# An opening computed feature chunk by feature chunk, and projections spread over the attention steps

## The chip, the cores and the metric

The kernel runs on one core of a Trainium2 chip. The metric is the device time of one execution in microseconds (us); three runs of the kernel before gave 2430.28, 2433.61 and 2434.09 us, so the median is 2433.61 us. The engines are named as the profile names them: PE multiplies matrices and PEld loads its weights, DVE works on vectors, ACT evaluates functions, POOL is the general engine, and SP issues most of the transfers.

## The reference, cut to what matters

Two networks run one after the other. The change lies in the first one, a transformer of two layers over 256 tokens `x` and 256 context tokens `ctx`, 1024 features each. All values are 32-bit floats.

```python
for l in range(DEPTH):                       # DEPTH = 2
    with_ctx = l < DEPTH - 1
    mod_x = (silu_c @ w_ada[l] + b_ada[l])[:, None, :]      # six modulation vectors of 1024
    mod_c = (silu_cc @ w_ada[l] + b_ada[l])[None, None, :]
    sh1_x, sc1_x, gt1_x, sh2_x, sc2_x, gt2_x = jnp.split(mod_x, 6, axis=-1)
    ...
    hx = modulate(rms_norm(x, g_norm1[l]), sh1_x, sc1_x)    # h * (1 + scale) + shift
    hc = modulate(rms_norm(ctx, g_norm1[l]), sh1_c, sc1_c)
    qa, ka, va, qb, kb, vb, qc, kc, vc = jnp.split(hx @ w_in[l], bounds, axis=-1)
    ...                                      # the same for hc; three kinds of attention: a, b, c
    x = x + gt1_x * (jnp.concatenate([oa, ob, oc], axis=-1) @ w_out[l])
    hx2 = modulate(rms_norm(x, g_norm2[l]), sh2_x, sc2_x)
    x = x + gt2_x * conv_ffn(hx2, w_up[l], conv_w[l], conv_b[l], w_down[l])
    ...                                      # the same for ctx while with_ctx
```

The second network (two layers of feed-forward, attention, linear attention, feed-forward) takes `x` from there.

## The kernel before, in words

Features lie on the 128 partitions in eight chunks, tokens lie along the free dimension; both streams together make 512 columns. Every large product runs in three parts: `weight` (L254) loads a 512 KB weight tile, ACT rounds it to a high part (L261), DVE makes the low part (L262), and `mm1` (L265) issues the products high by high, high by low and low by high at L269, L270 and L271. One output tile of 128 features over eight chunks is therefore 24 matmuls.

*Opening* (`first`, from L791 on). SP loads the streams H and C, constants and vectors, and then `w_ada`. `ada` (L362) is a generator of steps: one step loads 512 KB of `w_ada` into one of the four weight buffers and multiplies it by the two condition vectors (L372); eight steps make one of the six modulation vectors of a layer. Sixteen steps, the shift and the scale of layer 0, run in the opening. ACT squares both streams (L339), DVE and POOL add them, PE sums them over the partitions (L350, L351), ACT and DVE make the factor of the norm (L315 to L324). DVE multiplies the streams by it (L820, L821), and when the sixteenth step is through, `modulate` (L417) makes the inputs of the projections.

*Projections and attention* (`first_layer`). Layer l has 18 projection tiles, in the order of `IN1` (L56). `gemm` (L279) runs the first three chunk by chunk side by side and the next three one after the other; `done` then normalises each query or key tile (L447 to L458, with a sum by PE at L450) or transposes values (L468). Tiles 6 to 17 come from the generator `project`. Eight attentions follow: two of kind c, two of kind b, four of kind a. An attention consists of steps: scores on PE (L528 for c, L531 and L532 for the others), a maximum on DVE (L478), exponentials on ACT (L480), a scaling on ACT (L491), transposes on PE (L551, L569), copies on DVE (L554), and at its end the product with the values (L579, L586). In layer 0 an attention has 6 steps, in layer 1 it has 4. Each step calls `fill` once: a projection while any are left, and after that a step of `ada`. After the attentions come the output projection, the second norm, and the feed-forward stage, whose 41 later tiles each call one more step of `ada`.

What sets the order: the program is written as above, and a scheduler then lines up each engine's instructions, with an eye to free buffers (four for weights, 33 named `n`, 18 named `q`, five PSUM banks `mm`, three PSUM banks `at`). On the chip each engine runs its line in order.

Of the kernel before, what the change touches and what calls it, by code (L numbers as in the profile page):

```python
# [9 lines left out]
F32 = mybir.dt.float32  # L10
# [29 lines left out]
_CON = [("ident", 128), ("ones", 128), ("ones128", 128), ("bd64", 128), ("bd32", 128), ("causal", 128)]  # L40
# [15 lines left out]
IN1 = ("kc", "vc", "qc", "kc", "vc", "qc", "kb", "vb", "qb", "kb", "vb", "qb", "ka", "va", "qa", "qa", "qa", "qa")  # L56
LEVELS = (64, 32, 16, 8, 4, 2, 1)


def _constants():  # L60
# [25 lines left out]
    put("causal", np.where(i[None, :] <= i[:, None], 0.0, MASKED))  # L86
    m = np.zeros((P, 8, P), np.float32)
# [10 lines left out]
def prep(v):  # L98
# [14 lines left out]
    d["w_ada"] = f(v["w_ada"])  # L113

# [71 lines left out]
class Kern:  # L186
# [92 lines left out]
    def gemm(self, tiles, done, head=3, hook=None, order=None, fill=None, ws=None):  # L279


        order = order or range(KC)
        ws = ws or [self.weight(t[0]) for t in tiles[:head]]
        pss = [self.mmp()[:, :t[2]] for t in tiles[:head]]
        for i, k in enumerate(order):
            for w, ps, t in zip(ws, pss, tiles):
                self.mm1(ps, w, k, t[1][k], i == 0, i == KC - 1)
        if hook:
            hook()
        for i, ps in enumerate(pss):  # L290
            done(i, ps)
# [125 lines left out]
    def modulate(self, l, v, gain, streams, zs, n, xn=None):  # L417
# [3 lines left out]
        for c in range(KC):  # L421
            hi, lo = self.n(F32R), self.n(F32R)
            if xn:
                t = self.t()[:, :512]
                for part, _ in streams:
                    u = slice(part * 256, (part + 1) * 256)
                    g, sh = gain[:, c, part:part + 1], self.mod(l, v, c, part)
                    nc.scalar.activation(hi[:, u], xn[c][:, u], AF.Identity, scale=g, bias=sh)
                    nc.vector.tensor_scalar(t[:, u], xn[c][:, u], g, sh, ALU.mult, ALU.add)
                nc.vector.tensor_tensor(lo, t, hi.bitcast(F32), ALU.subtract)  # L430
                xs.append((hi, lo))
                continue
# [173 lines left out]
    def first_layer(self, l):  # L606
# [7 lines left out]
        zs, head = None, self.head  # L614
        if not wc:
# [4 lines left out]
        xs = self.modulate(l, 0, self.G1[l], both, zs, 512, self.xn if wc else None)  # L620
        cut = {n: [(h[:, :n], o[:, :n]) for h, o in xs] for n in (256, 512)}
# [29 lines left out]
        self.gemm(tiles[:6], done, ws=head)  # L651
# [10 lines left out]
        self.project = project()  # L662
# [19 lines left out]
        order = []  # L682
        for j in range(2):
# [107 lines left out]
    def first(self, ctx):  # L791
# [15 lines left out]
        st = [self.stat_new(256, nc.vector), self.stat_new(256)]  # L807
# [3 lines left out]
        self.G1, self.G2 = {}, {}  # L811
        self.known, self.mods = -1, self.ada()
        for i in range(16):
            next(self.mods)
            if i == 7:
                with self.tc.issue_after(self.last_ada):
                    zs = [self.stat_end(s) for s in st]
                self.xn = [self.n() for _ in range(KC)]
                for c in range(KC):
                    nc.vector.tensor_tensor(self.xn[c][:, :256], self.H[:, c, TM:TH], zs[0], ALU.mult)  # L820
                    nc.vector.tensor_tensor(self.xn[c][:, 256:], self.C[:, c, :], zs[1], ALU.mult)  # L821
        self.head = [self.weight(A["w1_in"][0, j]) for j in range(3)]
        nc.sync.dma_start(self.CON1, A["con1"])
        nc.sync.dma_start(self.LAM, bass.AP(A["lamv"].tensor, 0, [[0, P], [1, 256]]))
# [476 lines left out]
_INS = ["hT", "cT", "ccT", "w_ada", "w1_in", "w1_out", "w1_up", "w1_dn", "w2_in", "w2_fg", "w2_out", "w2_up1", "w2_dn1",  # L1301
# [19 lines left out]
```

## Time and profile before

| | us |
|---|---|
| median of three runs | 2433.61 |
| the profiled execution | 2433.39 |
| its span, first to last instruction | 2431.6 |
| PE busy | 2320.8 (95%) |
| DVE busy | 1523.2 (63%) |
| ACT busy | 1270.2 (52%) |
| POOL busy | 401.7 (17%) |

The execution's own time is 1.8 us longer than the span. An engine's busy time is the time in which at least one of its instructions runs; PE's counts a matmul until it has left the array, so PE can be busy and still have gaps between starts. "Idle" below is the length of a stretch less the busy time.

### The profile page before, as it was taken

How to read it: one execution, taken by the hardware profiler on the slowest of the kernel's cores; microseconds unless marked ns; L12 is line 12 of the kernel's file. 1: busy time of each engine (PE TensorE's matmuls, PEld its weight loads, DVE VectorE, ACT ScalarE, POOL GpSimd, SP SyncE). 2: the span in 40 equal slices, each digit the busy share in tenths (PEclk: the TensorE clock that was granted, in tenths of full speed). 3: DMA queues.
4: the chain of work that ended last, by engine and by line, in shares of the span. 5: the costliest groups of instructions: out<-in, count | busy, mean ns of one | idle time of the engine just before them, and what ended most of it. 6: DMA issues, size and time to landing. Idle time of an engine off the chain costs nothing. (4 is left out here: it accounts for less than half of the span.)

```text
span 2431.6 us, 40872 instructions
## 1 busy us (share of the span) xinstructions
PE 2320.8 (95%) x16128; PEld 2043.5 (84%) x16128; DVE 1523.2 (63%) x2605; ACT 1270.2 (52%) x2196; POOL 401.7 (17%) x417
## 2 busy tenths in 40 slices
PE   5999999999999989999999999899999999998998
PEld 3665677778877758999999988899989999888997
DVE  4667665444547776776664876676466557666664
ACT  3658644333346775664444545554454444466553
POOL 0300021000022001211111320321121122113111
PEclk8999999999999999999999999999999999999999
DMA  7313335433233246556555533445545545334653
GB/s 269 103 37 131 113 130 173 139 121 96 93 117 120 71 156 211 194 177 191 183 168 180 167 106 105 148 157 174 174 148 178 169 147 195 104 114 149 196 180 118
DMA packets 100993, 358.57 MB, mean 147 GB/s; under 512 B 11488, under 2 KB 12864, under 8 KB 100544
## 3 DMA queue, kind: packets, MB, share of 16 engines
q1 hardware_dynamic: 98640, 349.82, 44.4%
q0 software_dynamic: 1792, 5.53, 0.9%
q8 instruction: 127, 2.08, 0.4%
q10 hardware_dynamic: 368, 0.59, 0.1%
q14 instruction: 66, 0.54, 0.1%
HBM read 354.83 MB, written 1.07 MB: 146 GB/s over the span
## 5 line engine op out<-in xcount | busy, mean ns | idle before, releaser
L269 PE MATMUL mm_t<-n_t,hi_t 128*128 128x272 f32 (+2 forms) x3600 | 1112.4, 310 | 25.4 <-ACT n_t L839 18.7
L270 PE MATMUL mm_t<-n_t,hi_t 128*128 128x272 f32 (+2 forms) x3600 | 1109.5, 308 | 6.0 <-DVE n_t L840 5.0
L271 PE MATMUL mm_t<-n_t,lo_t 128*128 128x272 f32 (+2 forms) x3600 | 1106.0, 308 | 1.1 <-DVE lo_t L262 1.1
L262 DVE TENSOR_TENSOR lo_t<-raw_t,hi_t 128x1024 fp32r<-128x1024 f32 (+1 forms) x574 | 713.2, 1246 | 391.2 <-ACT hi_t L261 387.1
L261 ACT ACTIVATE hi_t<-raw_t 128x1024 fp32r<-128x1024 f32 (+1 forms) x574 | 595.5, 1039 | 680.6 <-PE mm_t L270 509.4
L269 PEld LDWEIGHTS mm_t<-n_t,hi_t 128*128 128x128 f32 x3600 | 686.0, 191 | 77.7 <-ACT n_t L839 20.9
L270 PEld LDWEIGHTS mm_t<-n_t,hi_t 128*128 128x128 f32 x3600 | 688.5, 191 | 38.1 <-DVE n_t L840 8.4
L271 PEld LDWEIGHTS mm_t<-n_t,lo_t 128*128 128x128 f32 x3600 | 687.9, 191 | 33.0 <-issue 5.8
L269 PE MATMUL mm_t<-q_t,hi_t 128*128 128x272 f32 (+2 forms) x896 | 274.6, 307 | 0.7 <-ACT q_t L306 0.7
L270 PE MATMUL mm_t<-q_t,hi_t 128*128 128x272 f32 (+2 forms) x896 | 274.4, 306 | 0.0
L271 PE MATMUL mm_t<-q_t,lo_t 128*128 128x272 f32 (+2 forms) x896 | 274.3, 306 | 0.0
L343 POOL TENSOR_TENSOR t_t<-t_t 128x272 f32<-128x272 f32 (+1 forms) x108 | 122.9, 1143 | 540.2 <-ACT t_t L339 515.2
L269 PEld LDWEIGHTS mm_t<-q_t,hi_t 128*128 128x128 f32 x896 | 168.4, 188 | 8.8 <-ACT q_t L306 1.1
L270 PEld LDWEIGHTS mm_t<-q_t,hi_t 128*128 128x128 f32 x896 | 168.9, 188 | 7.6 <-DVE q_t L307 0.2
L271 PEld LDWEIGHTS mm_t<-q_t,lo_t 128*128 128x128 f32 x896 | 168.9, 189 | 7.5
L888 POOL TENSOR_TENSOR t_t<-t_t 128x272 f32<-128x272 f32 (+1 forms) x88 | 75.6, 860 | 443.3 <-DVE t_t L882 386.9
L738 POOL TENSOR_TENSOR t_t<-t_t 128x512 f32<-128x512 f32 (+1 forms) x44 | 56.7, 1288 | 442.2 <-ACT t_t L737 442.2
L882 DVE TENSOR_TENSOR t_t<-mm_t,t_t 128x272 f32<-128x272 f32 (+1 forms) x176 | 75.6, 436 | 64.2 <-PE mm_t L271 62.4
L372 PE MATMUL at_t<-raw_t,CS 128*32 128x256 f32 x768 | 70.6, 431 | 35.7 <-DMA raw_t<-in_w_ada_dram 35.4
L307 DVE TENSOR_TENSOR q_t<-t_t,q_t 128x272 fp32r<-128x272 f32 (+2 forms) x112 | 55.8, 498 | 73.4 <-ACT q_t L306 73.4
L306 ACT ACTIVATE q_t<-t_t 128x272 fp32r<-128x272 f32 (+2 forms) x112 | 52.3, 467 | 90.4 <-POOL t_t L738 47.8
L480 ACT ACTIVATE t_t<-mm_t,s_t 128x512 f32<-128x512 f32 (+1 forms) x120 | 72.7, 607 | 26.5 <-DVE s_t L478 25.7
(253 smaller groups left out, 2146.9 us busy)
## 6 DMA issues: line engine op xcount, KB each, us to landing
raw_t<-in_w_up_dram SPq DMA_DIRECT2D x264, 512.0 KB, 3.3
raw_t<-in_w_in_dram SPq DMA_DIRECT2D x118, 512.0 KB, 3.4
raw_t<-in_w_ada_dram SPq DMA_DIRECT2D x96, 512.0 KB, 4.4
raw_t<-in_w_dn_dram SPq DMA_DIRECT2D x96, 448.0 KB, 3.3
raw_t<-in_w_dn_dram SPq DMA_DIRECT2D x48, 512.0 KB, 3.6
raw_t<-in_w_out_dram SPq DMA_DIRECT2D x32, 512.0 KB, 3.4
raw_t<-in_w_fg_dram SPq DMA_DIRECT2D x16, 512.0 KB, 3.3
q_t<-cum POOLq DMA_DIRECT2D x8, 272.0 KB, 7.4
```

The source lines that it names most:

```text
L261: nc.scalar.activation(hi[:, :k], raw[:, :k], AF.Copy)
L262: nc.vector.tensor_tensor(lo[:, :k], raw[:, :k], hi[:, :k].bitcast(F32), ALU.subtract)
L269: self.nc.tensor.matmul(ps, wh, xh, start=start, stop=False)
L270: self.nc.tensor.matmul(ps, wh, xl, start=False, stop=False)
L271: self.last_mm = self.nc.tensor.matmul(ps, wl, xh, start=False, stop=stop).ins
L307: self.nc.vector.tensor_tensor(lo, src, hi.bitcast(F32), ALU.subtract)
L343: st.eng.tensor_tensor(st.acc, st.acc, sq, ALU.add)
L372: self.last_ada = nc.tensor.matmul(ps[32 * g:32 * g + 32], self.CS[:, k, :], wv[:, g], start=k == 0, stop=k == KC - 1).ins
L480: nc.scalar.activation(pm[:, i * nk:(i + 1) * nk], sp[:, i * nk:(i + 1) * nk], AF.Exp, bias=m[:, i:i + 1], accum_out=sm[:, i:i + 1])
L738: nc.gpsimd.tensor_tensor(u, u, g, ALU.mult)
L882: nc.vector.tensor_tensor(u, ps, z[0], ALU.mult)
L888: nc.gpsimd.tensor_tensor(u, u, g, ALU.mult)
```

## The change

There are three parts.

The first two modulations of layer 0 are no longer steps of `ada`. The host lays their part of `w_ada` out anew (`w_ada0`), so that 1 MB holds all that one chunk of 128 features needs of shift and scale. `ada_chunk` loads it in four transfers of 256 KB into `q` buffers and multiplies it (L436); `mod_chunk` turns the result onto the partitions by a small product with a selecting matrix (L447), makes shift and gain for this chunk, and applies norm and modulation in one pass. Two chunks are loaded ahead of H and C; the other six stand behind the first four weight tiles. `gemm` gets a `feed` that prepares a chunk just ahead of its products, and four tiles instead of three run side by side. Both streams' squares are added on DVE.

Projections in the attention are issued at the steps of the table `DUE` alone; every other step is a step of `ada`, and in layer 0 these run ahead into layer 1's modulations. In layer 0 two projections (tiles 6 and 7) run before the first attention.

```diff
+DUE = ((2, 4, 6, 8, 10, 12, 15, 18, 21, 28, 34, 40), (1, 2, 4, 5, 6, 8, 10, 12, 14, 18, 22, 26))
...
+    a = v["w_ada"][0, :, :2048].reshape(4, 2, P, 2, KC, P)
+    d["w_ada0"] = f(a.transpose(4, 0, 2, 1, 3, 5).reshape(KC, 4, P, 512))
...
         for i, k in enumerate(order):
+            if feed:
+                feed(k)
             for w, ps, t in zip(ws, pss, tiles):
                 self.mm1(ps, w, k, t[1][k], i == 0, i == KC - 1)
...
-        for l, v in ((l, v) for l in range(2) for v in range(6)):
+        for l, v in ((l, v) for l in range(2) for v in range(2 * (1 - l), 6)):
...
-        if next(self.project, None) is None:
-            self.ada_step(l, 4)
+        self.step += 1
+        if not (self.step in DUE[l] and next(self.project, None)):
+            self.ada_step(*(1, 1) if l == 0 else (1, 4))
...
+    def ada_chunk(self, c):
...
+        ps = self.atp()[:, :256]
+        for h in range(2):
+            ws = [self.q()[:, :512] for _ in range(2)]
+            for i, w in enumerate(ws):
+                self.last_dma = nc.sync.dma_start(w, self.A["w_ada0"][c, 2 * h + i]).ins
+            for g in range(4):
+                self.last_ada = nc.tensor.matmul(ps[32 * g:32 * g + 32], self.CS[:, 4 * h + g, :],
+                                                 ws[g // 2][:, g % 2 * 256:(g % 2 + 1) * 256], start=h == 0, stop=h == 1).ins
+        e = self.t()[:, :256]
+        nc.scalar.activation(e, ps, AF.Copy)
+        return e
+
+    def mod_chunk(self, c, e):
...
+        m = self.atp()[:, :4].rearrange("p (v s) -> p v s", v=2)
+        for v in range(2):
+            nc.tensor.matmul(m[:, v], e[:, v * P:(v + 1) * P], self.con("sel"), start=v == 0, stop=v == 1)
+        o, _ = _VOFF["b_ada"]
+        for v in range(2):
+            nc.vector.tensor_scalar(self.MOD[0][:, v * KC + c], m[:, v], self.VEC[:, o + v * KC + c:o + v * KC + c + 1], None,
+                                    ALU.add)
+        gain = self.G1[0]
+        nc.vector.tensor_scalar(gain[:, c], self.MOD[0][:, KC + c], 1.0, self.gh[:, c:c + 1], ALU.add, ALU.mult)
+        hi, lo, t = self.n(F32R), self.n(F32R), self.t()[:, :512]
+        for part, src in enumerate((self.H[:, c, TM:TH], self.C[:, c, :])):
+            u, sh = slice(part * 256, (part + 1) * 256), self.mod(0, 0, c, part)
+            nc.vector.scalar_tensor_tensor(t[:, u], src, gain[:, c, part:part + 1], self.zs[part], ALU.mult, ALU.mult)
+            nc.scalar.activation(hi[:, u], t[:, u], AF.Identity, bias=sh)
+            nc.vector.scalar_tensor_tensor(lo[:, u], t[:, u], sh, hi[:, u].bitcast(F32), ALU.add, ALU.subtract)
+        return hi, lo
...
+            def feed(k):
+
+                while len(sums) < min(k + 2, KC):
+                    sums.append(self.ada_chunk(len(sums)))
+                x = self.mod_chunk(k, sums[k])
...
+        if wc:
+            for _ in range(2):
+                next(self.project)
...
-        nc.sync.dma_start(self.H, A["hT"])
-        nc.sync.dma_start(self.C, A["cT"])
         nc.sync.dma_start(self.CON, A["con"])
-        nc.sync.dma_start(self.VEC, A["vec"])
...
+        self.sums = [self.ada_chunk(c) for c in range(2)]
+        with self.tc.issue_after(self.last_dma):
+            nc.sync.dma_start(self.H, A["hT"])
+            nc.sync.dma_start(self.C, A["cT"])
+            last = nc.sync.dma_start(self.VEC, A["vec"]).ins
+        st = [self.stat_new(256, nc.vector), self.stat_new(256, nc.vector)]
...
+        with self.tc.issue_after(last):
+            self.head = [self.weight(A["w1_in"][0, j]) for j in range(4)]
```

How the lines of instructions move is shown at three places, PE each time. Lines 269 to 271 of the kernel before are lines 275 to 277 after; `at_t` and `mm_t` are PSUM banks, and `CS` holds the two condition vectors.

PE before, from the sums of the norm to the first projection products:

```order
L350 MATMUL at_t<-t_t,CON 128x256
L351 MATMUL at_t<-t_t,CON 128x256
L372 MATMUL at_t<-raw_t,CS 32x256 x32
L269 MATMUL mm_t<-n_t,hi_t 128x512
L270 MATMUL mm_t<-n_t,hi_t 128x512
L271 MATMUL mm_t<-n_t,lo_t 128x512
```

PE after, the same stretch:

```order
L358 MATMUL at_t<-t_t,CON 128x256
L359 MATMUL at_t<-t_t,CON 128x256
L447 MATMUL at_t<-CON,t_t 128x2 x2
L436 MATMUL at_t<-q_t,CS 32x256 x8
L447 MATMUL at_t<-CON,t_t 128x2 x2
L436 MATMUL at_t<-q_t,CS 32x256 x6
L447 MATMUL at_t<-CON,t_t 128x2 x2
L436 MATMUL at_t<-q_t,CS 32x256 x2
L275 MATMUL mm_t<-n_t,hi_t 128x512 x3
L276 MATMUL mm_t<-n_t,hi_t 128x512
```

The second modulation's eight steps have left the place ahead of the first products; in their stead stand the sums of chunks 2 and 3 alone.

PE after, where the products of chunk 2 end and those of chunk 3 begin (before, the products of all eight chunks follow each other here):

```order
L277 MATMUL mm_t<-n_t,lo_t 128x512
L436 MATMUL at_t<-q_t,CS 32x256 x8
L447 MATMUL at_t<-CON,t_t 128x2 x2
L436 MATMUL at_t<-q_t,CS 32x256 x8
L447 MATMUL at_t<-CON,t_t 128x2 x2
L436 MATMUL at_t<-q_t,CS 32x256 x8
L447 MATMUL at_t<-CON,t_t 128x2 x2
L436 MATMUL at_t<-q_t,CS 32x256
L275 MATMUL mm_t<-n_t,hi_t 128x512 x2
```

The sums of chunks 4, 5 and 6 and an eighth of chunk 7's stand together in the middle of the products; the rest of chunk 7's stands ahead of the products of chunk 6.

PE before, in the first attention of kind b, layer 0, after its scores:

```order
L595 MATMUL at_t_1629<-t_t_1625,CON_81 128x512
L372 MATMUL at_t_1675<-raw_t_1676,CS_94 32x256 x4
L372 MATMUL at_t_1675<-raw_t_1701,CS_94 32x256 x4
L372 MATMUL at_t_1675<-raw_t_1728,CS_94 32x256 x4
L532 MATMUL mm_t_1743<-q_t_1652,q_t_1644 128x512
```

PE after, in the same attention (L566 and L567 are the scores; `mm_t_1650` is projection tile 14):

```order
L566 MATMUL mm_t_1630<-q_t_1561,q_t_1555 128x256
L567 MATMUL mm_t_1630<-q_t_1563,q_t_1555 128x256
L275 MATMUL mm_t_1650<-n_t_265,hi_t_1645 128x512
L276 MATMUL mm_t_1650<-n_t_266,hi_t_1645 128x512
L277 MATMUL mm_t_1650<-n_t_265,lo_t_1646 128x512
```

Where only steps of `ada` filled the line before, products of a projection now stand too. Counted over PE's whole line of layer 0, the steps of `ada` are 24 in the attentions, 6 in the wait of the second norm and 18 in the feed-forward stage before, and 38, 2 and 8 after. From the feed-forward stage of layer 1 on both lines are the same.

## Rows read from the trace of the kernel before

**Rows 1.** The page, busy us of each engine.
```profile
PE 2320.8 (95%) x16128; PEld 2043.5 (84%) x16128; DVE 1523.2 (63%) x2605; ACT 1270.2 (52%) x2196; POOL 401.7 (17%) x417
```

**Rows 2.** Stretches: length; busy PE, PEld, DVE, ACT, POOL; clock, DMA share, GB/s.
```profile
0.00:43.10 43.10, 17.02 (x137) 5.78 (x137) 15.03 (x51) 13.67 (x31) 4.82 (x10) 0.82 0.85 301
43.10:62.80 19.70, 18.79 (x74) 14.84 (x74) 14.53 (x30) 11.78 (x21) 0.00 (x0) 0.88 0.49 172
62.80:82.40 19.60, 19.60 (x83) 14.60 (x82) 13.29 (x20) 13.33 (x21) 4.76 (x4) 1.00 0.43 135
82.40:199.50 117.10, 109.47 (x488) 74.96 (x487) 78.72 (x161) 75.58 (x156) 21.39 (x24) 0.99 0.17 50
199.50:294.30 94.80, 86.67 (x631) 54.45 (x631) 73.71 (x175) 79.98 (x188) 1.41 (x2) 0.98 0.45 156
333.20:344.00 10.80, 7.99 (x62) 3.76 (x60) 7.37 (x19) 6.54 (x14) 0.00 (x0) 0.88 0.61 221
762.60:826.60 64.00, 60.29 (x295) 42.51 (x294) 47.53 (x99) 43.22 (x87) 17.03 (x18) 1.00 0.29 91
826.60:857.00 30.40, 26.54 (x204) 22.54 (x203) 21.41 (x56) 25.40 (x57) 4.69 (x7) 1.00 0.16 53
857.00:917.20 60.20, 56.34 (x405) 35.79 (x404) 43.07 (x114) 42.37 (x89) 1.42 (x2) 0.94 0.52 175
```

**Rows 3.** The same view, three stretches of the opening.
```profile
5.00:10.00 5.00, 0.00 (x0) 0.00 (x0) 0.00 (x0) 1.14 (x4) 0.00 (x0) 1.00 1.00 412
25.00:30.00 5.00, 4.58 (x39) 2.69 (x38) 2.35 (x8) 2.61 (x6) 0.00 (x0) 0.76 0.66 228
45.00:50.00 5.00, 5.00 (x16) 3.96 (x17) 5.00 (x10) 4.11 (x8) 0.00 (x0) 0.71 1.00 337
```

**Rows 4.** Timeline of the opening: start, length, instruction, idle time before.
```profile
9.28 0.42 ACT L339 ACTIVATE t_t<-C 128x256 f32<-128x256 f32 x1 [2.08 <-DMA C<-in_cT_dram]
...
13.97 0.42 ACT L339 ACTIVATE t_t<-C 128x256 f32<-128x256 f32 x1 [0.30 <-DVE t_t L343]
...
24.13 1.22 PE L350 MATMUL at_t<-t_t,CON 128*128 128x256 f32 x2
...
29.97 0.42 DVE L324 SCALAR_TENSOR_TENSOR t_t<-t_t 128x256 f32<-128x256 f32 x1
...
40.64 0.38 ACT L377 ACTIVATE t_t<-at_t 128x256 f32<-128x256 f32 x1 [11.45 <-PE at_t L372]
...
43.10 0.79 PE L269 MATMUL mm_t<-n_t,hi_t 128*128 128x512 f32 x1 [2.52 <-ACT n_t L428]
```

**Rows 5.** Timeline of PE: a projection, then two `ada` steps in layer 0's feed-forward.
```profile
180.10 0.40 PE L269 MATMUL mm_t<-n_t,hi_t 128*128 128x512 f32 x1
...
183.28 0.39 PE L271 MATMUL mm_t<-n_t,lo_t 128*128 128x512 f32 x1
...
365.41 0.64 PE L372 MATMUL at_t<-raw_t,CS 128*32 128x256 f32 x8
...
371.65 0.64 PE L372 MATMUL at_t<-raw_t,CS 128*32 128x256 f32 x8
```

**Rows 6.** Groups by line, PE, 199.5 to 294.3 us: count, busy, mean, idle before.
```profile
L372 PE MATMUL at_t<-raw_t,CS 128*32 128x256 f32 x192 | 16.3, 386 | 2.4 <-DMA raw_t<-in_w_ada_dram 2.3 <-DVE n_t L307 0.2
```

**Rows 7.** Waits of PE: us in total, times, longest; layer 0, then layer 1.
```profile
PE at_t L450 <- ACT t_t L447: 4.7, 6, 1.6
...
PE at_t L372 <- DMA raw_t<-in_w_ada_dram: 2.3, 5, 0.7
...
PE at_t L551 <- ACT t_t L491: 3.6, 2, 3.1
```

**Rows 8.** Groups by line, ACT and DVE, 82 to 294 us.
```profile
L261 ACT ACTIVATE hi_t<-raw_t 128x1024 fp32r<-128x1024 f32 x13 | 13.7, 1055 | 11.8 <-PE mm_t L270 11.6 <-DMA raw_t<-in_w_out_dram 0.2
L315 ACT ACTIVATE t_t<-at_t,eps 128x512 f32<-128x512 f32 x12 | 8.3, 688 | 6.5 <-PE at_t L450 5.5 <-PE at_t L595 0.8
L317 ACT ACTIVATE t_t<-t_t 128x512 f32<-128x512 f32 x12 | 7.5, 625 | 0.2
L320 DVE SCALAR_TENSOR_TENSOR t_t<-at_t,t_t 128x512 f32<-128x512 f32 x12 | 8.3, 690 | 6.2 <-ACT t_t L317 6.2
```

More of the change, by code (lines that the diff above doesn't have):

```diff
@@ L37 @@
 NVEC = _n
-_CON = [("ident", 128), ("ones", 128), ("ones128", 128), ("bd64", 128), ("bd32", 128), ("causal", 128)]
+_CON = [("ident", 128), ("ones", 128), ("ones128", 128), ("bd64", 128), ("bd32", 128), ("causal", 128), ("sel", 2)]
 _COFF = {}
@@ L86, in _constants @@
     put("causal", np.where(i[None, :] <= i[:, None], 0.0, MASKED))
+    put("sel", i[:, None] % 32 == np.arange(2)[None, :])
     m = np.zeros((P, 8, P), np.float32)
@@ L277, in mm, with gemm @@
             self.mm1(ps, w, k, xs[k], first and i == 0, last and i == len(xs) - 1)
-    def gemm(self, tiles, done, head=3, hook=None, order=None, fill=None, ws=None):
+    def gemm(self, tiles, done, head=3, hook=None, order=None, fill=None, ws=None, feed=None):
         order = order or range(KC)
@@ L415, in mod_gain, with modulate @@
         return a
-    def modulate(self, l, v, gain, streams, zs, n, xn=None):
+    def ada_chunk(self, c):
+        nc = self.nc
+        ps = self.atp()[:, :256]
[10 more added lines that the diff above has]
+    def mod_chunk(self, c, e):
+        nc = self.nc
+        m = self.atp()[:, :4].rearrange("p (v s) -> p v s", v=2)
[14 more added lines that the diff above has]
+        return hi, lo
+    def modulate(self, l, v, gain, streams, zs, n):
         nc = self.nc
@@ L422, in modulate @@
             hi, lo = self.n(F32R), self.n(F32R)
[L423 to L432, printed above, removed]
             for part, src in streams:
@@ L613, in first_layer @@
         both = ((0, X), (1, C))
-        zs, head = None, self.head
-        if not wc:
+        head, feed = self.head, None
+        cut = {256: [], 512: []}
+        if wc:
+            sums = self.sums
+            def feed(k):
+                while len(sums) < min(k + 2, KC):
+                    sums.append(self.ada_chunk(len(sums)))
+                x = self.mod_chunk(k, sums[k])
+                for n in cut:
+                    cut[n].append(tuple(a[:, :n] for a in x))
+        else:
             head = [self.weight(A["w1_in"][l, j]) for j in range(3)]
@@ L619, in first_layer @@
                 self.ada_step(l, 4)
-        xs = self.modulate(l, 0, self.G1[l], both, zs, 512, self.xn if wc else None)
-        cut = {n: [(h[:, :n], o[:, :n]) for h, o in xs] for n in (256, 512)}
+            for x in self.modulate(l, 0, self.G1[l], both, zs, 512):
+                for n in cut:
+                    cut[n].append(tuple(a[:, :n] for a in x))
         gains = {}
@@ L650, in first_layer, with late @@
         tiles = [(A["w1_in"][l, i], cut[n], n) for i, n in enumerate(ns)]
-        self.gemm(tiles[:6], done, ws=head)
+        def late():
+            with self.tc.issue_after(self.last_dma):
+                nc.sync.dma_start(self.CON1, A["con1"])
+        self.gemm(tiles[:6], done, ws=head, head=len(head), feed=feed,
+                  hook=late if wc else None)
         def project():
@@ L660, in project @@
                 yield True
-        self.project = project()
+        self.project, self.step = project(), 0
         def get(nm, j):
@@ L682, in first_layer @@
         order = []
+        if wc:
+            for _ in range(2):
+                next(self.project)
         for j in range(2):
@@ L800, in first @@
         nc.sync.dma_start(cs, A["ccT"].rearrange("p c i -> p (c i)"))
-        nc.sync.dma_start(self.H, A["hT"])
-        nc.sync.dma_start(self.C, A["cT"])
         nc.sync.dma_start(self.CON, A["con"])
-        nc.sync.dma_start(self.VEC, A["vec"])
         nc.scalar.activation(self.CS.rearrange("p c i -> p (c i)"), cs, AF.Silu)
         self.table_exp()
-        st = [self.stat_new(256, nc.vector), self.stat_new(256)]
+        self.sums = [self.ada_chunk(c) for c in range(2)]
+        with self.tc.issue_after(self.last_dma):
+            nc.sync.dma_start(self.H, A["hT"])
+            nc.sync.dma_start(self.C, A["cT"])
+            last = nc.sync.dma_start(self.VEC, A["vec"]).ins
+        st = [self.stat_new(256, nc.vector), self.stat_new(256, nc.vector)]
         for c in range(KC):
@@ L810, in first @@
             self.stat_add(st[1], self.C[:, c, :])
[L811 to L824, printed above, removed]
+        self.zs = [self.stat_end(s) for s in st]
+        with self.tc.issue_after(last):
+            self.head = [self.weight(A["w1_in"][0, j]) for j in range(4)]
+        self.G1, self.G2 = {0: p1.tile([P, KC, 2], F32, name="gain_g_norm1_0")}, {}
+        self.gh = p1.tile([P, KC], F32, name="gh")
+        nc.vector.tensor_scalar(self.gh, self.vec(0, "g_norm1", 0, KC), -0.5, None, ALU.mult)
+        self.known, self.mods = 1, self.ada()
+        nc.scalar.dma_start(self.LAM, bass.AP(A["lamv"].tensor, 0, [[0, P], [1, 256]]))
         self.first_layer(0)
@@ L1298, in build @@
             k.second(c2)
-_INS = ["hT", "cT", "ccT", "w_ada", "w1_in", "w1_out", "w1_up", "w1_dn", "w2_in", "w2_fg", "w2_out", "w2_up1", "w2_dn1",
+_INS = ["hT", "cT", "ccT", "w_ada", "w_ada0", "w1_in", "w1_out", "w1_up", "w1_dn", "w2_in", "w2_fg", "w2_out", "w2_up1", "w2_dn1",
         "w2_up2", "w2_dn2", "walpha", "vec", "lamv", "rpb", "con", "con1", "lmask"]
```

## The prediction

> **What bounds the kernel now.** I read the page's busy times first: PE is busy 2320.8 of 2431.6 us, DVE 63%, ACT 52% [rows 1]. So time can come from two places: PE's idle time, 110.8 us in all, and PE work that can be moved to where PE idles. Then I cut the span at the stages that the change touches and read their busy times [rows 2]. Up to the first projection product at 43.10 us PE is busy 17.02 us and the transfers run at a share of 0.85: this stretch waits for loads and for a chain over ACT and DVE. In the 231.5 us from 62.8 to 294.3 (three more tiles, then the attentions of layer 0) PE idles 0 + 7.63 + 8.13 = 15.8 us; in layer 1's attentions (762.6 to 917.2) 3.71 + 3.86 + 3.86 = 11.4 us. Last I read who ends PE's waits there: the squares of a projection on ACT, 4.7 us in 6 waits; steps of `ada` on their load, 2.3 us in 5; in layer 1 a scaling on ACT, once for 3.1 us [rows 7]. The reader is to see that projections stand only in the first attentions, and that PE is 93% busy there and 91% busy behind them all the same.
>
> The sum goes against the profiled execution, 2433.39 us (span 2431.6 plus 1.8 around it), which lies 0.2 us under the median of three runs.
>
> **Unit prices.** A tile's matmuls start 0.227 us apart (15 from 180.10 to 183.28 us, [rows 5]), so 24 take 5.45 us; with its small products a tile costs PE 19.60 / 3 = 6.5 us and ACT 13.33 / 3 = 4.4 us (the stretch of three tiles, [rows 2]). A step of `ada` between tiles of the feed-forward stage costs 6.24 - 5.45 = 0.79 us (365.41 to 371.65, one tile and one step, [rows 5]), in the attentions 16.3 / 24 = 0.68 us [rows 6].
>
> **1. The opening.** What was late: C was first read at 9.28 us, the last square ended at 14.39, PE's sums began only at 24.13, the norm's factors were ready at 30.39, and then everything waited for the second modulation until 40.64 [rows 4]. After, 8 MB of `w_ada` no longer stand ahead of the products, but 2.1 MB of it and the constants stand ahead of C: 4.79 MB up to C's end instead of 2.29. At 391 to 412 GB/s (the upper from [rows 3]) C comes 6.2 us later, at 15.5. The sixteen squares took 5.1 us: 20.6. The sums to both factors took 6.3 us: 26.9. ACT rounds four weight tiles in between, 1.05 us each [rows 8], three of them beside PE's sums: I add 1.5 us. From the modulation to the first product it was 2.5 us; I add 1 us for the selecting products, which wait for `at` banks that DVE frees. First product at 32, not 43.1; bounds 29 (the loads hidden, no bank wait) and 36 (all four roundings in the way).
>
> The products themselves are four tiles, 96 matmuls, in three pieces. The first 36 take 8.2 us and 2.4 more at the lower clock: before, PE had been sparsely busy, and the stretch from 45 to 50 us was granted 0.71, part at 1.2 and part at 2.4 GHz [rows 3]. I expect the same: 42.6. Then the sums of chunks 4 to 6 and the start of 7, 4.1 us by half the price above per 256 KB: 46.7. Another 36: 54.9. The rest of chunk 7, 1.3 us, and a chain like that before the first product, 2.5 us, in which PE idles: 58.7. The last 24: 64.1. Before, 72 matmuls were done at 62.8 and 24 more 6.5 us later, at 69.3. **Worth -5.2 us**; bounds -9 and +2.
>
> **2. Projections in layer 0's attentions.** Six of the twelve leave the attentions of kind c, two of them to a place just before, four to kinds b and a. The PE work is the same, so what counts is the idle time of 15.8 us. Half of the waits I expect to stay: the squares' waits come with every query or key tile wherever it stands, and the loads' waits with every step of `ada`; those two make 7.0 us. Of the other 8.8 us the new products cover half: **-4.4 us**. Bounds: -15.8 if all idle time goes, +12 if steps come so thin in kind c that each waits 1 us for its predecessor's chain.
>
> **3. Steps of `ada` in layer 0.** 14 more in the attentions, 14 x 0.68 = **+9.5 us**, since PE is over 90% busy there. 10 fewer in the feed-forward stage, 10 x 0.79 = **-7.9 us**. Four fewer in the wait of the second norm, where PE is idle 2.8 of 10.8 us anyway [rows 2]; the first products no longer stand behind the last of them: **-1 us**, bounds -2 and +2 (PE idles longer and may be granted 1.2 GHz for longer; this stretch already has 0.88).
>
> **4. Layer 1.** Four projections leave the third attention for the later ones, two go to it; the steps of `ada` keep their number. The stretch from 857.0, which has only scores and steps of `ada`, idles 3.86 us and was granted 0.94, so about 7 us of it at 1.2 GHz; the 3.1 us wait lies there. Products of projections stand in its place: **-4 us**, bounds -9 and +4.
>
> What I cost at nothing: twice as many transfers per megabyte of `w_ada0` on SP, covered since every issue is ahead of its need; the squares' adds, now all on DVE, which is idle there (28 of 43 us). SP's line ahead of the next weight tiles is longer by the six chunks, but the tiles' products come after the same chunks.
>
> Sum: -5.2 - 4.4 + 9.5 - 7.9 - 1 - 4 = -13.0. 2433.4 - 13.0 = **2420**.
>
> **Rivals.**
>
> *A, the forecast*, 2412 to 2430: PE is the bound in all attentions, and a moved instruction costs what it cost before. For it: 91% busy in kinds b and a [rows 2].
>
> *B, room behind PE.* ACT is busy 79.98 of 94.8 us in kinds b and a, and PE's weight loads only 54.45. If PE's busy time there is mostly latency, the four projections and eight of the extra steps cost not 26 + 5.4 = 31.4 us but what ACT needs, 4 x 4.4 = 17.6. Less 2.8 us that I have already counted as filled that is 11 us better: 2409. Against it: PE starts instructions right behind each other there, with waits of a few us in all. The Trainium skill speaks for B: Perfetto Trace Analysis, section Identifying the Most-Contended Engine, holds that PE's matmul busy share says little about headroom and that the weight loads' share is the one to read; the 57% and 91% of this stretch differ as that rule would have it, but no run here shows yet which of the two tells the room.
>
> *C, the opening stays bound by its loads.* When PE's buffers held the loads back, they ran at 228 GB/s [rows 3]. At that rate C is read at 22 us, the first product comes at 38.5, and the last chunk (13.5 MB in) lands at 61; its sum, chain and 24 matmuls end at 71, 2 us later than before: 2420 + 7 = 2427. For it: transfers of half the size. Against it: the loads were held back by four buffers, and there are 18 for the new ones. [...]
>
> *D, a wait for PSUM banks, slower.* A step's sum by `ada` holds one of three `at` banks through eight steps. Before, that was so only behind the projections; now it is so while projections are normalised. A norm's sum holds a second bank through three ACT operations and one on DVE, 0.69 + 0.63 (twice) + 0.69 = 2.6 us [rows 8], and the transposes of the scores, in PE's line behind it, have the last. There are 20 such tiles in both layers; at 1 us each, between nothing and 2.6, that is +20: 2440. It decides from 0.65 us per tile on. Against it: behind the projections, where `ada` holds a bank already, no wait for a bank is among PE's waits of [rows 7].
>
> That the change does not do what it says: PE's line shows the chunks in three pieces, not one by one; that is in the sum. The projections do stand at the table's steps.
>
> **Chances.** A 0.55, B 0.20, C 0.12, D 0.13. No change is within 0.2%, 4.9 us, about what a measurement of this kernel can tell. A is faster with 0.88 of its chance, B wholly, C in half, D never: 0.48 + 0.20 + 0.06 = 0.74 faster. The same: 0.12 of A, half of C, a tenth of D: 0.14. Slower 0.12. The range for 8 in 10 goes from 2405 (B and a little more; the far bound of part 2 is left out) to 2436 (C and the lower half of D).
>
> **What would show it.** Part 1: first L275 at 29 to 36 us, the last of the four tiles' products at 60 to 67. If C holds, PE waits for `w_ada0` with L436 after 45 us. Part 2: from there to the end of the attentions PE idles 9 to 13 us; under B the stretch of kinds b and a grows by under 20 us, under A by 25 to 32. Part 3: the feed-forward stage of layer 0 is 8 us shorter. Part 4: PE's long wait for a scaling in layer 1 is gone, and the clock there is at 1.00. Under D PE's products L485, L503 or L586 wait for DVE or ACT operations that read an `at` bank. The forecast is wrong if the attentions of layer 0 end earlier than the opening's gain explains, or later than at 300 us.

## The result, and the profile after

The kernel after takes 2460.64 us (median of four runs, 2460.17 to 2463.86) against 2431.95 us before in the same comparison: 1.0124 times as long, 95% interval 1.0104 to 1.0145. It is 28.7 us slower, and the forecast of 2420 was wrong in its sign. The profiled execution took 2463.86 us.

First the busy times of the profile after, to be held against [rows 1]. PE is busy 22.3 us longer, for 32 instructions more; PE's idle time, 119.0 us, is 8.2 us longer. The span is 30.5 us longer: 4.6 us up to the first scores of layer 1's attentions, 23.9 in these attentions and 2.0 behind them, where both kernels have the same lines.

```profile
PE 2343.1 (95%) x16160; PEld 2061.0 (84%) x16160; DVE 1526.8 (62%) x2622; ACT 1271.6 (52%) x2202; POOL 390.9 (16%) x411
```

Then the stretches of the profile after that answer to [rows 2]: length; busy PE, PEld, DVE, ACT, POOL with their instructions; clock, DMA share, GB/s. They are the time to the first product, the four tiles in two rows, the attentions of layer 0, the wait of the second norm, and layer 1's attentions in three rows and then as a whole.

```profile
0.00:34.95 34.95, 16.63 (x84) 8.37 (x84) 13.94 (x51) 16.21 (x35) 0.20 (x4) 0.74 0.94 354
34.95:58.00 23.05, 23.05 (x140) 17.15 (x140) 10.38 (x32) 5.97 (x14) 0.00 (x0) 0.95 0.45 174
58.00:70.60 12.60, 10.69 (x48) 8.27 (x48) 5.51 (x15) 4.60 (x9) 0.00 (x0) 0.73 0.00 1
...
97.90:349.30 251.40, 236.17 (x1348) 155.32 (x1348) 163.93 (x350) 161.74 (x357) 33.64 (x36) 0.98 0.38 122
349.30:356.50 7.20, 3.60 (x25) 1.76 (x23) 5.03 (x11) 4.90 (x11) 0.00 (x0) 1.00 0.42 138
767.20:862.00 94.80, 90.35 (x485) 62.27 (x484) 65.21 (x145) 66.06 (x136) 16.29 (x18) 0.98 0.30 89
862.00:930.00 68.00, 47.96 (x307) 32.18 (x308) 41.70 (x101) 39.25 (x82) 5.63 (x8) 0.79 0.41 139
930.00:962.00 32.00, 31.97 (x244) 29.20 (x240) 19.53 (x37) 15.99 (x29) 7.87 (x6) 0.98 0.30 99
767.20:962.00 194.80, 170.28 (x1033) 123.65 (x1032) 126.44 (x283) 121.29 (x246) 29.79 (x32) 0.91 0.34 109
```

The same view of the kernel before, for the whole attentions of layer 0 and of layer 1:

```profile
82.40:333.20 250.80, 235.04 (x1289) 161.62 (x1289) 168.49 (x357) 167.65 (x365) 37.11 (x38) 0.99 0.30 97
762.60:933.50 170.90, 159.45 (x1033) 116.90 (x1032) 124.61 (x283) 120.72 (x246) 31.29 (x32) 0.98 0.38 124
```

Layer 1's attentions are the place: 194.8 instead of 170.9 us, with 1033 instructions on PE in both. Of the 23.9 us, 13.1 are idle time (24.5 against 11.45) and 10.8 are longer busy time for the same work, at a lower clock (0.91 against 0.98). In kind a, from 862 to 930 us, PE is idle 20 of 68 us. Its waits in layer 1's attentions after (line waited for: us in total, times, longest) begin with

```profile
PE at_t L586 <- ACT t_t L526: 17.3, 4, 6.2
PE at_t L380 <- DMA raw_t<-in_w_ada_dram: 2.9, 2, 2.3
```

The first row is the wait that the forecast wanted gone [rows 7, the wait of 3.6 us]; it comes four times now, not twice. The clock's share shows in the stretches of kind a at the lower level (0.50, that is 1.2 GHz), with the one between the first two, in the same columns as above:

```profile
866.70:873.60 6.90, 4.23 (x17) 3.46 (x19) 4.15 (x11) 4.18 (x9) 1.33 (x2) 0.51 0.45 183
873.60:883.80 10.20, 7.31 (x52) 6.01 (x48) 6.44 (x17) 5.78 (x14) 0.46 (x1) 1.00 0.17 51
883.80:890.60 6.80, 4.51 (x15) 2.68 (x17) 3.36 (x12) 3.10 (x7) 0.95 (x2) 0.50 0.00 0
904.30:911.10 6.80, 6.18 (x26) 3.37 (x24) 3.19 (x8) 2.27 (x5) 0.00 (x0) 0.50 0.76 267
921.40:931.60 10.20, 5.80 (x22) 4.16 (x24) 6.19 (x13) 5.15 (x10) 1.41 (x2) 0.50 0.68 244
```

The kernel before has one such stretch in its attentions of layer 1:

```profile
863.70:870.50 6.80, 6.09 (x42) 3.48 (x43) 4.30 (x13) 6.66 (x16) 0.00 (x0) 0.50 0.27 83
```

PE waits from 863.9 to 869.4, 880.9 to 886.1 and 919.2 to 925.5 us. In each of these waits the clock goes down from 1.00 to 0.50, and it stays there beyond the wait's end; the stretch from 904.3 us begins behind a wait of 2.3 us for a load of `w_ada`. In these four stretches, and in 3.4 us from 778.1 us on, PE is busy 24.1 us at 1.2 GHz, against 6.1 us before. If this work takes half as long at 2.4 GHz, the clock accounts for some 9 of the 10.8 us (an estimate); what makes up the rest is not shown.

What PE waits for in the second of them is seen in the timeline of the kernel after (start, length, instruction, idle time before):

```profile
878.33 0.28 PE L277 MATMUL mm_t<-n_t,lo_t 128*128 128x256 f32 x1
...
879.37 0.63 PE L485 MATMUL at_t<-t_t,CON 128*128 128x256 f32 x2
879.65 0.59 PE L566 MATMUL mm_t<-q_t 128*128 128x512 f32 x1
880.04 0.47 ACT L323 ACTIVATE t_t<-at_t,eps 128x256 f32<-128x256 f32 x1 [0.42 <-PE at_t L485]
880.43 0.48 PE L567 MATMUL mm_t<-q_t 128*128 128x512 f32 x1
...
882.83 0.43 DVE L490 STREAM_SHUFFLE t_t<-q_t 128x256 f32<-128x256 f32 x1
883.16 0.68 DVE L513 TENSOR_REDUCE s_t<-mm_t 128x1 f32<-128x512 f32 x1
...
884.78 0.43 DVE L493 TENSOR_TENSOR q_t<-q_t,t_t 128x256 f32<-128x256 f32 x1 [0.94 <-POOL q_t L492]
...
885.32 1.33 ACT L526 ACTIVATE t_t<-t_t,s_t 128x512 f32<-128x512 f32 x2 [0.66 <-DVE s_t L523]
886.09 1.97 PE L586 MATMUL at_t<-CON,t_t 128*128 128x128 f32 x8 [5.18 <-ACT t_t L526]
886.82 0.84 ACT L545 ACTIVATE q_t<-q_t 64x256 fp32r<-64x256 f32 x2
888.15 0.42 DVE L548 TENSOR_TENSOR q_t<-q_t 64x256 fp32r<-64x256 f32 x1
889.04 0.80 PE L566 MATMUL mm_t<-q_t 128*128 128x512 f32 x1
```

The reader is to see two things. The last scores of an attention end at 880.9, but their maximum (L513) starts at 883.16: DVE's line first does the new query's norm and rotation (L328 to L490; their sum is L485 on PE), and L493 stands between the softmax's steps too. And PE has nothing else: the next attention's first scores (L566) start at 889.04, when the stack of that query (L548) is through, 10 us after the query's products end (L277, 878.6). The first gives theory Q1 (the chain stands ahead of the softmax), the second Q2 (PE lacks cover, since the next query comes too late). Both were called Q until the runs could tell them apart.

### The profile page after: what moved, and what is told of

Same layout as the page of the kernel before. It is cut to its first block, busy times and chain, and to the rows that moved or that the text cites. A ratio compares the mean times of both kernels' runs of the same rounds, so it can differ in the third digit from the quotient of the medians.

```text
span 2462.1 us, 40960 instructions
## 1 busy us (share of the span) xinstructions
PE 2343.1 (95%) x16160; PEld 2061.0 (84%) x16160; DVE 1526.8 (62%) x2622; ACT 1271.6 (52%) x2202; POOL 390.9 (16%) x411
## 5 line engine op out<-in xcount | busy, mean ns | idle before, releaser
L277 PE MATMUL mm_t<-n_t,lo_t 128*128 128x272 f32 (+2 forms) x3600 | 1107.6, 308 | 1.1 <-DVE lo_t L268 1.1
L277 PEld LDWEIGHTS mm_t<-n_t,lo_t 128*128 128x128 f32 x3600 | 688.3, 191 | 31.1 <-issue 3.9
L277 PE MATMUL mm_t<-q_t,lo_t 128*128 128x272 f32 (+2 forms) x896 | 274.1, 306 | 0.0
L351 POOL TENSOR_TENSOR t_t<-t_t 128x272 f32<-128x272 f32 (+1 forms) x102 | 118.1, 1163 | 455.9 <-ACT t_t L347 437.9
L277 PEld LDWEIGHTS mm_t<-q_t,lo_t 128*128 128x128 f32 x896 | 168.9, 188 | 7.7
L940 POOL TENSOR_TENSOR t_t<-t_t 128x272 f32<-128x272 f32 (+1 forms) x88 | 74.8, 851 | 445.5 <-DVE t_t L934 392.8
L934 DVE TENSOR_TENSOR t_t<-mm_t,t_t 128x272 f32<-128x272 f32 (+1 forms) x176 | 75.6, 436 | 66.1 <-PE mm_t L277 64.1
L513 DVE TENSOR_REDUCE s_t<-mm_t 128x1 f32<-128x512 f32 (+1 forms) x100 | 67.9, 681 | 29.9 <-PE mm_t L567 12.0
```

What stands on the lines that cost most here:

```text
L277: self.last_mm = self.nc.tensor.matmul(ps, wl, xh, start=False, stop=stop).ins
L351: st.eng.tensor_tensor(st.acc, st.acc, sq, ALU.add)
L513: nc.vector.tensor_reduce(m, sp.rearrange("p (s k) -> p s k", s=nseg), AX.X, ALU.max, negate=True)
L934: nc.vector.tensor_tensor(u, ps, z[0], ALU.mult)
L940: nc.gpsimd.tensor_tensor(u, u, g, ALU.mult)
```

## The experiments

Each row: median; ratio to the kernel before; first scores of kind c; end of layer 0's attentions; length of its feed-forward stage; length of layer 1's attentions. The last four are us read from the profiled execution, from the start of a stage's first score, or of the norm's sums that end it, to the next.

| kernel | median | ratio, 95% | c | end 0 | ffn 0 | att. 1 |
|---|---|---|---|---|---|---|
| before | 2431.3 to 2433.7 | | 82.4 | 333.2 | 387.1 | 171.0 |
| after | 2460.64 | 1.0104-1.0145 | 97.9 | 349.3 | 378.3 | 194.9 |
| e1_layer1_old | 2437.24 | 1.0008-1.0028 | 96.7 | 347.5 | 379.0 | 171.7 |
| e2_layer0_old | 2461.02 | 1.0101-1.0131 | 86.6 | 339.5 | 386.7 | 193.8 |
| e3_both_old | 2440.45 | 1.0021-1.0045 | 85.3 | 339.3 | 386.6 | 171.9 |
| e4_queries_early | 2443.57 | 1.0027-1.0055 | 96.4 | 348.1 | 378.8 | 175.8 |
| e5_ada_limit | 2461.99 | 1.0102-1.0136 | 96.5 | 342.5 | 385.5 | 192.4 |
| e6_open_three | 2432.11 | 0.9984-1.0007 | 78.9 | 334.4 | 386.7 | 171.8 |
| e8_copy_only | 2435.71 | 1.0005-1.0026 | 97.0 | 348.6 | 378.3 | 167.9 |
| e9_chain_later | 2467.63 | 1.0128-1.0162 | 95.5 | 346.4 | 378.2 | 198.3 |
| e10_no_ada | 2475.69 | 1.0166-1.0197 | 96.7 | 346.9 | 378.3 | 209.5 |
| e11_three_spread0 | 2431.52 | 0.9986-1.0010 | 92.2 | 342.1 | 378.9 | 173.1 |
| e12_three_ahead4 | 2433.08 | 0.9996-1.0016 | 78.5 | 331.5 | 386.8 | 172.3 |
| e13_one_earlier | 2442.96 | 1.0029-1.0059 | 97.0 | 348.4 | 378.1 | 175.4 |

### Which part costs: e1, e2, e3, e5

e1: `DUE[1]` = `tuple(range(1, 13))`.

> The changed kernel with layer 1's table put back (a projection at each of the first twelve steps). Theory Q (late queries: a query's norm, rotation and stacking stand in ACT's and DVE's lines ahead of a softmax that PE waits for): layer 1's attentions (first scores to end of the output projection) take 171 +- 4 us instead of 194.9, PE waits for no scaling over 3.5 us, total 2437 +- 4. Rival L (the loss in layer 1 comes from another alignment that the stage inherits, not from its table): the attentions stay near 190 us, total above 2452.

2437.24 us, layer 1's attentions 171.7 us: 23.4 us of the loss hang on layer 1's table alone, and rival L falls.

e2, layer 0 put back:

```diff
-DUE = ((2, 4, 6, 8, 10, 12, 15, 18, 21, 28, 34, 40), (1, ...
+DUE = (tuple(range(1, 13)), (1, ...
-            self.ada_step(*(1, 1) if l == 0 else (1, 4))
+            self.ada_step(l, 4)
-        if wc:
-            for _ in range(2):
-                next(self.project)
```

> The changed kernel with layer 0's attentions put back: a projection at each step until none is left, then ada up to layer 0's own, nothing run up front. Layer 1's table stays new. Theory P (PE is the bound: moved ada steps cost 0.68 us each, spreading costs a few us): attentions 14 us shorter, norm +1, feed-forward 8 us longer, total 2453 +- 5. Rival (the opening has delayed layer 0's attentions): attentions stay within 4 us, total 2465 or more. Layer 1's attentions stay near 195 us.

Missed: 2461.02, no change. The attentions end 9.8 us earlier, not 14, and the feed-forward stage takes 8.4 us more. What layer 0's part of the change takes it gives back.

e5, the middle edit of e2 alone:

> The changed kernel with layer 0's steps of ada bounded as before (up to its own modulations), the table of projections left as it is. Theory P: attentions 9.5 us shorter, norm +1, feed-forward 8 us longer: total 2460 +- 3. Rival W (ada steps in the attentions cost more than their 0.68 us, since they wait for loads and hold back the weight tiles behind them on the queue): attentions 14 us or more shorter, total 2455 or less.

2461.99, the total that P gives: the attentions end 6.8 us earlier, where P has 9.5, and the feed-forward stage is 7.2 us longer. Fourteen steps of `ada` cost about the same in either place.

e3, the edits of e1 and e2 together:

> The changed kernel with both layers' attentions put back as before, so that only the new opening is left of the change. If the parts add up (layer 1's table 23.4 us, layer 0's arrangement nothing in total, as the first four runs say): 2437 +- 3, and the first scores of kind c come at 86 to 87 us against 82.4 in the kernel before. Rival (the opening gains its 5 us, and the loss came from how it meets the new tables): 2430 or less.

2440.45, just above the range expected, first scores at 85.3 us: the opening by itself is slower than the one before, by 0.21% to 0.45%. Beside e1, layer 0's new arrangement is worth 3.2 us here (0.4 us beside the new table, e2); neither is clear of the noise, since the intervals of e1 and e3 overlap, and those of e2 and the kernel after.

### What the late queries cost: e4, e8, e9, e10, e13

e4: `DUE[1]` ends in `13, 14, 15, 16` instead of `14, 18, 22, 26`.

> The changed kernel, in layer 1 the last four queries of kind a at steps 13 to 16 (second attention of kind b) instead of 14, 18, 22 and 26; tiles 6 to 13 stay spread. Theory Q: the waits of 5.4, 5.2 and 6.2 us in kind a are gone, and with them the low clock there; layer 1's attentions 175 to 182 us, total 2444 +- 4. Rival D (an accumulator of ada holds an at bank while projections are normalised): ten tiles are still normalised under it, most of the loss stays, 190 us, total above 2454. Rival S (any spreading costs): half of the loss stays, 2450.

2443.57 us and 175.8 us, Q's numbers: four of twelve projections carry 17 of the 23.4 us. D, which needs only that `ada` runs beside projections, would have left 190, and S half of the loss. What the other 6 us hang on was not tried.

e8:

```diff
                 self.mm(ps, w, xx)
-                done(i, ps)
+                if l == 1 and i > 13:
+                    o = self.q()
+                    nc.scalar.activation(o[:, :n], ps, AF.Copy, scale=gains["gq_a"])
+                    T["qa"].append(o)
+                else:
+                    done(i, ps)
```

> The changed kernel, where layer 1's last four queries of kind a (tiles 14 to 17) are only copied with their gain: their norm and rotation are left out, the projections stay at steps 14, 18, 22 and 26. Theory Q (the chain of norm and rotation in ACT's and DVE's lines ahead of a softmax): the waits for a scaling over 3.5 us are gone, layer 1's attentions 173 to 181 us, total 2441 to 2447. Rival R (a projection among single ada steps leaves PE without other work, whatever follows it, for instance since it holds one of five mm banks): two of the three long waits stay, total 2452 or more.

2435.71 us, layer 1's attentions 167.9 us, better than expected, with the products where they were and their `mm` bank held for one ACT operation less (L482, 0.4 us). So it is the chain behind the products that costs, and R falls. How much of that is the chain's place and how much its work, e8 cannot say: DVE is busy 8.8 us and ACT 6.0 us less in these attentions than in the kernel after. PE's waits in layer 1 in this kernel:

```profile
PE at_t L586 <- ACT t_t L526: 4.4, 4, 2.1
PE at_t L380 <- DMA raw_t<-in_w_ada_dram: 4.1, 2, 2.1
```

e9 puts the chain behind the next softmax (lines are three later here):

```diff
         self.step += 1
+        late, self.late = getattr(self, "late", None), None
+        if late:
+            late()
...
-                done(i, ps)
+                if l == 1 and i > 13:
+                    self.late = lambda i=i, ps=ps: done(i, ps)
+                else:
+                    done(i, ps)
```

> The changed kernel with the same computation, but norm and rotation of these four queries are written one attention step later, behind the next step's softmax; the projection's products stay in their place, and its mm bank is held for longer. Theory Q: the softmax goes first, the long waits shrink to under 2.5 us each, layer 1's attentions 176 to 184 us, total 2443 to 2450. Rival R (the mm bank): at least as slow as the changed kernel, 2458 or more. If the scheduler lines the chain up ahead of the softmax all the same, the time stays and the lines of ACT and DVE show it.

2467.63 us, slower still: the forecast from Q failed. The waits for the softmax shrink as it says, though not to 2.5 us, but the next attention's scores (here L569) now wait for their query's stack (L551):

```profile
PE at_t L589 <- ACT t_t L529: 9.3, 7, 3.5
PE mm_t L569 <- DVE q_t L551: 7.2, 1, 7.2
```

R had this time too, but for the bank, which e8 excludes. This run split Q into Q1 and Q2: the softmax's place mattered less than when the query is ready.

e13: `DUE[1]` ends in `13, 14, 18, 22`.

> The changed kernel, in layer 1 each of the four queries of kind a one attention earlier: steps 13, 14, 18 and 22 instead of 14, 18, 22 and 26. Two of them still stand in kind a, each ahead of a softmax, but the next attention's query is always there. Theory Q2 (what is missing is cover: PE's line has no further scores to put ahead of the transposes, since their query is still in its chain): no wait for a scaling over 2.5 us, layer 1's attentions 173 to 179 us, total 2440 to 2446. Theory Q1 (the chain's place ahead of the softmax is enough): at the two queries that still stand in kind a the waits stay at 4 to 6 us each, attentions 184 to 190 us, total 2451 to 2457.

2442.96 us, 175.4 us: Q2, and Q1 misses by 8 us or more. Two queries still stand in kind a with their whole chain, ahead of a softmax as before (on DVE L490 at 884.67, L513 at 885.01, L493 at 886.66 us), and no wait for a scaling is over 0.9 us. A single wait of 4.7 us (scores for a stack) is left; it stands ahead of the first attention of kind a, whose query (step 13) is the only one that is still projected in the attention right before its use. PE's timeline in e13, around the first of the two:

```profile
880.88 0.64 PE L485 MATMUL at_t<-t_t,CON 128*128 128x256 f32 x2
881.35 0.60 PE L586 MATMUL at_t<-CON,t_t 128*128 128x128 f32 x4
...
882.03 0.50 PE L566 MATMUL mm_t<-q_t 128*128 128x512 f32 x1
...
885.94 0.39 PE L566 MATMUL mm_t<-q_t 128*128 128x512 f32 x1
...
887.97 1.31 PE L586 MATMUL at_t<-CON,t_t 128*128 128x128 f32 x8 [0.69 <-ACT t_t L526]
```

The sum L485 and the eight transposes stand at the same places of the program as in the timeline after; between them stand further scores and, from 883 to 886, the next projection. That needs their query to be there.

e10 (lines are three later):

```diff
-            self.ada_step(*(1, 1) if l == 0 else (1, 4))
+            if l == 0:
+                self.ada_step(1, 1)
+            elif self.step < 14:
+                self.ada_step(1, 4)
```

> The changed kernel, in which layer 1 issues no step of ada from attention step 14 on; they all run at the end of the attentions instead, bound by their loads, so the total is 10 to 25 us longer. What counts is kind a, up to its last product with the values. Rival D (an at bank held by ada's sum): the waits of transposes for a scaling are gone there. Q1 and Q2: they stay, three or four of 5 us or more.

2475.69 us; in kind a (862 to 937 us) PE waits

```profile
PE at_t L589 <- ACT t_t L529: 24.2, 6, 5.3
```

against 16.9 us in 3 waits in kind a after. Without `ada`'s sums in their banks the waits are more: D falls, and the steps of `ada` are cover, not the cause.

### The opening: e6, e11, e12

e6: as e3, with `range(3)` instead of `range(4)` for the tiles' weights in `first`.

> As e3_both_old, but three tiles side by side in the opening instead of four. Theory F (four tiles keep all weight buffers until 70 us, the transfers stand still from 45 to 70 us, the fifth and sixth tiles' weights come late and PE idles and loses its clock at 82 to 91 us): the transfers run on before 70 us, the first scores of kind c come at 83 us, total 2433 +- 3. Rival G (three tiles give PE too little between the chunks' chains): the products wait longer for the chunks, total 2437 or more.

2432.11 us, 8.3 less than e3, level with the kernel before. The total is F's (the first scores, at 78.9 us, come 4 us earlier than F has them), the cause is not. Transfers do stand still in e3 (6 GB/s from 45 to 60 us, 23 from 60 to 70; in e6 37 and 186), but PE waits for no weights. Its waits from 30 to 100 us in e3 begin with

```profile
PE mm_t L275 <- ACT n_t L458: 1.9, 1, 1.9
PE at_t L485 <- ACT t_t L482: 1.4, 1, 1.4
PE mm_t L563 <- DVE q_t L493: 1.4, 1, 1.4
```

a chunk's chain and twice a projection's. What F says of the clock holds: from 82.4 to 95 us it is 0.73 in e3 and 0.95 in e6. The same 38 us of e3, then of e6 (columns as above; PE's busy time and clock):

```profile
32.00:70.00 38.00, 36.09 (x196) 26.55 (x196) 17.78 (x50) 12.36 (x25) 0.00 (x0) 0.89 0.37 141
```

```profile
32.00:70.00 38.00, 38.00 (x206) 27.68 (x205) 24.06 (x58) 16.41 (x30) 0.00 (x0) 0.95 0.51 185
```

With three tiles PE has no gap here, and six tiles are through at 77.1 instead of 81.4 us; the first scores come 6.4 us earlier. G falls.

e11 (e1 and three tiles):

> The changed kernel with three tiles side by side in the opening and layer 1's table put back; layer 0's new table and its ada steps stay. If the parts add up: e1's 2437 less the 8.3 us that three tiles gave = 2429, 3 us below the kernel before. Rival: two projections ahead of the first attention make up for the fourth tile by themselves, so three tiles give less here: 2434 or more.

2431.52 us: neither faster nor slower than before, and between the two numbers expected (2429, and 2434 or more). e12 (e6, and `min(k + 4, KC)` in `feed`):

> As e6_open_three, and the sums of four chunks instead of two run ahead of the chunk that is fed. If the products' three pieces are what the opening loses on (idle between them and the lower clock behind it): first scores of kind c 1 to 3 us earlier than 78.9, total 2430. Rival: more sums ahead of the first product make it later, and nothing is gained: 2432 or more.

2433.08 us, the same, as the rival has it. The first scores come only 0.4 us earlier than in e6, though layer 0's attentions end 2.9 us earlier. No version beat the kernel before by what can be measured. Single executions differ by 5 us behind layer 1's attentions alone (1496.7 us in e13, 1502.0 in e9), so gains of 2 us by stage, as e12's, stay open.

## Why the prediction was wrong

**Part 4 failed, and carries most of the miss.** It put layer 1 at -4 us, at most +4: "Products of projections stand in its place", namely of a wait of 3.1 us. Measured: +23.9, of which e1 takes back 23.2. That is 28 of the 42 us between the forecast of -13.0 and the 28.7 measured. The step counted a late query as PE work that fills a gap. But a query is work that others wait for: 10 us pass from its last product to the first scores that use it. While it is on its way PE cannot run ahead into the next attention, and what had covered the softmax in the kernel before was just that. The trace of before had the numbers: `ada`'s products fill only 13.5 of the 60.2 us of kind a (128 of them), and yet PE idles 3.86 us [rows 2]; the rest had to be attention steps that run ahead. Rows of the kernel before, the group first, then the timeline:

```profile
L372 PE MATMUL at_t<-raw_t,CS 128*32 128x256 f32 x128 | 13.5, 449 | 0.5 <-DMA raw_t<-in_w_ada_dram 0.5
...
883.71 0.39 PE L531 MATMUL mm_t<-q_t 128*128 128x512 f32 x1
884.03 1.95 PE L579 MATMUL at_t<-n_t,q_t 128*64 128x256 f32 x16
```

L579 ends an attention, and the scores right ahead of it (L531, L532 and L531 from 883.15 us on) are the next one's. I read the stretch as one with a gap to fill. The sign would have been wrong without part 4 too: e1, which has the old table in layer 1, is still 0.08% to 0.28% slower than the kernel before.

**Part 1 was mis-sized, and out of its bounds.** It was put at -5.2 us, between -9 and +2; e3, in which only the opening is left of the change, is 0.21% to 0.45% slower than the kernel before, some 5 to 11 us. The first product came at 34.95 us, within the bounds. The transfers of 256 KB ran at 387 GB/s, and PE waits for no load of `w_ada0` after 45 us, so rival C falls; that it has the four tiles done at 71 us, close to the 70.6 measured, is luck. The Trainium skill asks for 1 MiB or more per DMA for the highest bandwidth (DMA: Bandwidth & Descriptors, Rules for kernel authors). Here that does not decide: transfers of 512 KB ran at 391 GB/s from 10 to 15 us of the kernel before, 1% faster than those of 256 KB, and the 412 GB/s of [rows 3] belong to H, C and the constants, of up to 1088 KB. The rows of the kernel after (timeline):

```profile
22.22 1.22 PE L358 MATMUL at_t<-t_t,CON 128*128 128x256 f32 x2 [8.69 <-DVE t_t L351]
...
28.35 1.93 PE L436 MATMUL at_t<-q_t,CS 128*32 128x256 f32 x16 [1.71 <-DVE t_t L328]
...
34.95 1.65 PE L275 MATMUL mm_t<-n_t,hi_t 128*128 128x512 f32 x3
...
62.04 2.08 PE L275 MATMUL mm_t<-n_t,hi_t 128*128 128x512 f32 x4 [1.91 <-ACT n_t L458]
```

and, of the same kernel, a stretch in which only such transfers ran (GB/s in the last column):

```profile
25.00:30.00 5.00, 3.29 (x23) 1.97 (x21) 4.86 (x11) 3.38 (x9) 0.00 (x0) 0.50 1.05 387
```

In the kernel before, the stretch of 512 KB transfers, and the last product of the fourth tile:

```profile
10.00:15.00 5.00, 2.28 (x20) 0.55 (x24) 4.68 (x20) 4.09 (x13) 4.22 (x6) 1.00 1.02 391
...
68.74 0.39 PE L271 MATMUL mm_t<-n_t,lo_t 128*128 128x512 f32 x1
```

The four tiles were done at 70.6 us, not 64.1: 3 us from the start (2.1 of them since C was first read at 17.64 us and not at 15.5), 3.1 in the last piece (8.5 instead of 5.4 us, at a lower clock, behind an idle time of 1.91 us), the rest in `ada`'s sums. In the kernel before the fourth tile ended at 69.1 us, so the 8 us earlier start bought nothing. What came behind was in no term: in e3, where the rest is as before, six tiles are through at 81.4 us, 1.1 earlier than before, but the first scores wait for the norms of the last tiles, and come 2.9 us later than before. That four tiles ending together is the reason fits e6, which changes their number alone; it was not tried by itself. Where the rest of e3's 5 to 11 us arises is open.

**Parts 2 and 3 came out near nothing in sum, and not in their terms.** The forecast was -4.4 + 9.5 - 7.9 - 1 = -3.8; the medians say -0.4 (e2) to -3.2 (e1 against e3), and in the profiled executions the feed-forward stage ends 1.4 us (beside e2) and 0.6 us (e1 beside e3) later with the new arrangement. None of this is clear of the noise. Part 3's norm and feed-forward stage are 8.8 us shorter (378.3 for 387.1), where 8.9 was forecast. A step of `ada` in the attentions takes PE 27.3 / 38 = 0.72 us after, 0.68 was used. But from the four tiles to the last product with the values (70.6 to 305.7 us) PE idles 15.9 us, where 9 to 13 was forecast and 15.8 was before: part 2's -4.4 did not come. That end lies behind 300 us, which was named as a sign of being wrong. The squares' waits went, as wished, and one of 4.6 us of scores for their query's stack (L566 for L548) came, layer 1's mechanism at a smaller size; that this row is its whole price in layer 0 was not tried.

**The rivals.** D was the only rival on the slow side, 20 us short of the result, but its mechanism is refuted (e4, e10); PE's L586 waited for a scaling, which reads no `at` bank. Between A and B the sign that was named for them speaks for A: the stretch of kinds b and a in layer 0 takes 125.5 us where it took 94.8, 30.7 more, and A has 25 to 32, B under 20. In the kernel after it is

```profile
180.20:305.70 125.50, 113.36 (x765) 72.59 (x763) 85.35 (x196) 94.30 (x211) 5.70 (x8) 0.96 0.42 140
```

The runs agree in part: the 14 steps of `ada` that e5 takes out, 14 x 0.72 = 10.1 us of PE, gave 6.8 us back in a single profiled execution, so some two thirds of them were not hidden. The room that the weight loads' share of 57% would promise (the Trainium skill, Perfetto Trace Analysis, Identifying the Most-Contended Engine) was there for a third.

## What to carry to other kernels

Before spreading work over later gaps, ask for each piece when the last operation that its consumer waits for is through, not when its products are. Here a query needed 10 us from its last product to its first use, and most of the loss went when it was projected one attention earlier than the one before its use. An engine that is 91% busy with short instructions may be so because it runs ahead; whatever makes the next stage's input late takes the cover away, and the wait shows up at another instruction, in another operation's name. And tiles that accumulate side by side end together: count from there to the first use of the last of them, not from the first product.

## What was not expected of the hardware

A wait cost more than its own length. In each of three waits of 5.2 to 6.2 us the granted clock fell to 0.50, for 6.8 to 10.2 us, and by the estimate above work at that level makes up some 9 of layer 1's 23.9 us. In the kernel before, the one wait of 3.1 us there came with a single such stretch, 6.8 us at 0.50 (863.7 to 870.5 us).
